# Input projection of a two-layer hybrid backbone: the low halves of the weights formed on VectorE, and the PSUM copies and head-norm steps given a place 100 instructions earlier in the planner's order

## The chip, the cores and the metric

The kernel runs on one core of one Trainium2 chip. The metric is device time in microseconds (us) of one execution of the whole program; lower is better. The program is one launch: both layers, the attention, the long convolution, the feed-forward and the last norm.

## What the reference computes

Two trunk layers run over 1152 tokens of width 1024: 128 context tokens and 1024 latent tokens, each group with its own modulation. What matters here is the first half of a layer:

```python
h = _rms_norm(x, p['norm1']) * (1 + sc1) + sh1
proj = h @ p['w_in']                                   # 1024 -> 2048 columns
q, k, v, zc, zh = jnp.split(proj, IN_SPLITS, axis=-1)  # 512, 128, 128, 512, 768
q = _rms_norm(q.reshape(b, L, N_HEADS, HEAD_DIM), p['q_norm'])
k = _rms_norm(k.reshape(b, L, N_KV_HEADS, HEAD_DIM), p['k_norm'])
q = _rope_2d(q, rows, cols); k = _rope_2d(k, rows, cols)
attn_out = _blocked_attention(q, keys, vals)
conv_out = _conformer_conv(zc, p)     # a * sigmoid(gate), 31 taps, group norm, silu, projection
hy_out = _hyena(zh, p)                # 3-tap conv, then two long convolutions with gates
x = x + g1 * (jnp.concatenate([attn_out, conv_out, hy_out], axis=-1) @ p['w_o'])
```

The other half is a feed-forward of width 2816 with a 3-tap convolution. All of it is float32.

## The kernel before

**Precision.** Every large matrix product is made of three products of rounded halves (`mm3`): high weight by high activation, high weight by low activation, low weight by high activation. A weight piece of 128x512 is loaded by a DMA of SyncE's queue into `raw` (two buffers), ScalarE casts it to `whi`, and an engine named by `self.wl_eng` subtracts to get `wlo` (four buffers each; `wload`, lines 257 to 265). `wqueue` issues the load of a piece two pieces ahead of its use.

**Stage.** `phase1` is the input projection of a layer. The 2048 columns are 16 blocks `m` of 128, taken in the order 10 to 15 (the long convolution's inputs), 0 (q), 4 (k), 5 (v), 1 (q), 8, 6, 9, 7 (the gated convolution's two pairs), 2, 3 (q). A block takes two weight pieces; its result is three PSUM tiles of 384 tokens (`dense`, or `normed_dense2` for the first two blocks, where the norm of the input is worked out segment by segment). In `phase1`, `self.wl_eng` is GpSimd; `phase3` and `phase4` set it to VectorE.

**What follows a block.** Blocks 10 to 15 are copied by ScalarE into one padded row `raw` (`short`, four copies, after three GpSimd memsets of the padding) and run through three taps into `zs`. Blocks 0 to 4 are squared and scaled by ScalarE out of PSUM (`nsq`, `nw`), head sums are made on TensorE (`s`, `sums64`), ScalarE takes the root and VectorE the reciprocal (`nsd`), TensorE spreads it (`nr`, `bcast64`) and VectorE multiplies (`nw`); `rope_out` follows, with two products on GpSimd. Block 5 is copied out (`vraw`). Blocks 8 and 9 go through a tanh (`th`), and with 6 and 7 still in PSUM VectorE forms the product (`do_glu`). The tiles of `s` and `nr` share a single PSUM buffer (`self.A`); the projection's own PSUM ring has four tiles.

**Beside it.** Between the parts of a block, `tick` takes one step of the head norms (`post`) and one of the long convolution (`bg`: `hyena`, two transforms of a chain of VectorE additions and products between TensorE products `ft`, `xp`, `iy`). In layer 0 the filter's transform (`pre`) runs first. After block 9 the long convolution is run to its end, its memory is given up, and `open_attention` takes the memory for keys and queries; `maxes(0)`, the first stage of the attention, runs beside blocks 7, 2 and 3.

**Order.** The program is written once in this order; a planner then gives each engine its own in-order list, from a simulated timeline. Among instructions that are ready in that timeline the one that stands earliest in the program goes first, and `tc.high_priority(offset=n)` makes an instruction count as n places earlier. Nothing is reordered on the chip: each engine takes its list in order.

Of the kernel before, what the change touches and what calls it, by code (L numbers as in the profile page):

```python
# [11 lines left out]
AF = mybir.ActivationFunctionType  # L12
ALU = mybir.AluOpType
# [109 lines left out]

SIDE_TAPS = 10

ORDER = [([10, 11, 12, 13, 14, 15, 0, 4, 5, 1, 8, 6, 9, 7, 2, 3], 9), ([10, 11, 12, 13, 14, 15, 0, 4, 5, 1, 8, 6, 9, 7, 2, 3], 9)]

MX_LAG = 1
# [6 lines left out]
class Kern:  # L135
# [87 lines left out]

    def stt(self, out, a, s, b, op0, op1, eng=None):
        return (eng or self.nc.vector).scalar_tensor_tensor(out, a, s, b, op0=op0, op1=op1)  # L225

    def hilo(self, hi, lo, src, hi_eng="act", lo_eng=None):

        if hi_eng == "act":
            self.nc.scalar.copy(hi, src)  # L230
        else:
            hi_eng.tensor_copy(hi, src)
        self.tt(lo, src, hi.bitcast(F32), ALU.subtract, lo_eng)
# [487 lines left out]
    def short(self, l, m, ts):  # L721

        nc, v = self.nc, self.vec[l]
        raw = self.hs.tile([128, 1156], F32, tag="raw", name="raw", bufs=1)
        nc.gpsimd.memset(raw[:, 0:1], 0.0)
        nc.gpsimd.memset(raw[:, 129:130], 0.0)
        nc.gpsimd.memset(raw[:, 1154:1155], 0.0)
        nc.scalar.copy(raw[:, 1:129], ts[0][:, 0:128])
        nc.scalar.copy(raw[:, 130:386], ts[0][:, 128:384])
        nc.scalar.copy(raw[:, 386:770], ts[1][:, 0:384])  # L730
        nc.scalar.copy(raw[:, 770:1154], ts[2][:, 0:384])
        z = self.hs.tile([128, 1156], F32, tag="zs", name="zs", bufs=3)
        w = V_SW + 3 * m
        self.act(z[:, :1153], raw[:, 1:1154], AF.Identity, scale=v[:, w + 1 : w + 2], bias=v[:, V_SB + m : V_SB + m + 1])
        self.stt(z[:, :1153], raw[:, 0:1153], v[:, w : w + 1], z[:, :1153], ALU.mult, ALU.add)
        self.stt(z[:, :1153], raw[:, 2:1155], v[:, w + 2 : w + 3], z[:, :1153], ALU.mult, ALU.add)
        self.dump(f"z{l}", z[:, :1153], lambda d: d[:, m, :])
        return z
# [323 lines left out]
    def normed(self, l, ts, w, scale, eps, done, dst):  # L1062

        nc, ms, qs = self.nc, [], []
        for s, t in enumerate(ts):
            q = self.N("nsq", "nsq", 3)
            self.act(q[:], t[:, :384], AF.Square)
            qs.append(q)
            m = self.N("nw", "nw", 4)
            self.act(m[:], t[:, :384], AF.Copy, scale=w)  # L1070
            ms.append(m)
        yield
        sd = self.small([128, 9, 2], "nsd")
        self.act(sd[:], self.sums64(qs), AF.Sqrt, scale=scale, bias=eps)
        nc.vector.reciprocal(sd[:], sd[:])
        yield
        for s in range(3):
            R = self.bcast64(sd, 3 * s, 3 * s + 3, "nr")
            self.mul(ms[s][:], ms[s][:], R[:, :384])
            if s == 0:  # L1080
                done(ms[0][:, 0:128])
            self.rope_out(l, ms[s], s, dst)
            yield
# [20 lines left out]
    def do_v(self, l, ts):  # L1104
        nc = self.nc

        ms = []
        for s in range(3):
            m = self.N("vraw", "nw", 4)
            nc.scalar.copy(m[:], ts[s][:, :384])  # L1110
            ms.append(m)
        nc.sync.dma_start(self.o["nv"][l], ms[0][:, 0:128])
        yield
        blocks = [(s, b) for s in range(3) for b in range(3)]
        for g in ((0,), (1, 2, 3, 4), (5, 6, 7, 8)):
            t = self.A("vt")
            for k, n in enumerate(g):
                s, b = blocks[n]
                self.tr(t[:, 128 * k : 128 * k + 128], ms[s][:, 128 * b : 128 * b + 128])
            if len(g) == 1:  # L1120
                m = self.M("vp")
                nc.scalar.copy(m[:, :128], t[:, :128])
                nc.sync.dma_start(self.vpD[:], m[:, :128])
            else:
                m = self.M("vs")
                nc.scalar.copy(m[:], t[:])
                nc.sync.dma_start(self.vD[:, g[0] - 1 : g[0] + 3].rearrange("p b g e -> p (b g e)"), m[:])
            yield

    def do_gate(self, ts):  # L1130
        ms = []
        for t in ts:
            m = self.N("th", "nw", 4)
            self.act(m[:], t[:, :384], AF.Tanh, scale=0.5)
            ms.append(m)
        return ms

    def do_glu(self, l, c, th, ta):

        for s, (a, b) in enumerate(SEG):  # L1140
            self.stt(th[s][:], th[s][:], 1.0, ta[s][:, :384], ALU.add, ALU.mult)
            self.nc.sync.dma_start(self.uD[c, :, a:b], th[s][:])

    def open_short(self):
# [3 lines left out]
    def phase1(self, l, x, pre):  # L1148

        nc = self.nc  # L1150
        with ExitStack() as ctx:
            with self.tc.high_priority(offset=P4_PRIO[0] + 40):
# [1 line left out]
                hp = self.pool(ctx, f"h{l}", 8)  # L1154
                hh = [hp.tile([128, NT], F32R, tag="hh", name="hh") for _ in range(8)]
                hl = [hp.tile([128, NT], F32R, tag="hl", name="hl") for _ in range(8)]
            self.wl_eng = nc.gpsimd
            self.rp = self.pool(ctx, f"rp{l}", 1)
            main = self.ring(ctx, f"p{l}", 2, 4)
            self.use(main)  # L1160
            order, end = ORDER[l]
            w = self.wqueue([self.i["w_in"][l, m, h] for m in order for h in range(2)])
# [9 lines left out]
            for k, m in enumerate(order):  # L1172
                ts = next(two) if k < 2 else self.dense(w, hh, hl, "win", tick=tick)
# [696 lines left out]
```

## Time and profile before

| | us |
|---|---|
| three timed runs: lowest, median, highest | 3380.13, 3380.18, 3384.11 |
| the profiled execution, its own time | 3374.35 |
| span of that execution's trace | 3372.2 |
| TensorE matmul busy in the span | 3159.7 (94%) |
| VectorE busy | 2166.0 (64%) |
| ScalarE busy | 1193.9 (35%) |
| GpSimd busy | 626.8 (19%) |

Around the span lie 3374.35 - 3372.2 = 2.15 us. TensorE's busy time is the sum of pipelined matmuls and not a measure of peak; what counts below is the time in which it has nothing at all, and the granted clock. Layer 0's projection runs from about 88 to 394 us, layer 1's from about 1760 to 2048 us.

### The profile page before, as it was taken

What the parts mean: (1) busy time and instruction counts of PE and PEld (TensorE: products, weight loads), DVE (VectorE), ACT (ScalarE), POOL (GpSimd) and SP (SyncE); (2) the same over time, 40 slices, a digit from 0 to 9 for tenths busy, and PEclk for the clock granted to TensorE, in tenths of its full rate; (3) what the DMA queues carried; (4) which work ended last, traced back from release to release, by engine and by line L of the source; (5) the groups of instructions that cost most, each with busy time, mean ns of one, the idle gap of its engine ahead of it and who ended that gap; (6) DMA issues with size and microseconds to landing.
All of it is one profiled execution on the core that took longest, in us unless ns stands there. A gap on an engine that the chain in (4) does not pass through costs nothing.

```text
span 3372.2 us, 44662 instructions
## 1 busy us (share of the span) xinstructions
PE 3159.7 (94%) x17330; PEld 2782.6 (83%) x17330; DVE 2166.0 (64%) x3398; ACT 1193.9 (35%) x1978; POOL 626.8 (19%) x478
## 2 busy tenths in 40 slices
PE   5999778999899999999999998889999999999997
PEld 3899733459799999999999995335799999999997
DVE  7878799665765545455477786897356444554556
ACT  3433333452342223333344333335334233333323
POOL 6533324231210000000024333332110000000002
PEclk8899879999899999999999997889999999999998
DMA  7565544544311111111123536341511111111112
GB/s 284 172 210 184 144 155 165 172 149 155 125 38 42 44 42 44 41 45 41 44 79 104 188 116 207 109 152 51 197 32 48 41 43 43 41 44 41 41 45 69
DMA packets 152327, 336.08 MB, mean 100 GB/s; under 512 B 21360, under 2 KB 57844, under 8 KB 145589
## 3 DMA queue, kind: packets, MB, share of 16 engines
q1 hardware_dynamic: 147412, 318.69, 29.5%
q0 software_dynamic: 4704, 14.55, 1.5%
q8 instruction: 137, 2.24, 0.3%
q14 instruction: 74, 0.60, 0.1%
HBM read 264.86 MB, written 68.31 MB: 99 GB/s over the span
## 4 chain that ended last, share of the span: by engine, by line
PE 72%; DVE 17%; DMA 6%; issue 2%; ACT 1%; POOL 1%; SPq 1%; DVEq 0%; ACTq 0%; POOLq 0%
PE up L236 32%; PE dn L236 16%; PE win L236 6%; PE wo L236 6%; DVE ca L225 3%; PE av L236 2%; PE st L236 2%; DVE mx L1343 2%; PE S L236 2%; DVE nt L225 1%; DMA q<-qD 1%; DVE Y L213 1%; PE fc L236 1%; DVE hl L225 1%; PE flt L236 1%
## 5 line engine op out<-in xcount | busy, mean ns | idle before, releaser
L236 PE MATMUL up<-hl,whi 128*128 128x384 f32 (+1 forms) x2112 | 713.1, 338 | 4.2 <-DVE hl L225 3.4
L236 PE MATMUL up<-hh,whi 128*128 128x384 f32 (+1 forms) x2112 | 711.0, 338 | 3.6 <-ACT hh L210 2.7
L236 PE MATMUL up<-hh,wlo 128*128 128x384 f32 (+1 forms) x2112 | 712.0, 337 | 0.0
L213 DVE TENSOR_TENSOR wlo<-wraw,whi 128x512 fp32r<-128x512 f32 x296 | 205.7, 695 | 626.1 <-ACT whi L230 623.7
L230 ACT CAST whi<-wraw 128x512 fp32r<-128x512 f32 x362 | 223.9, 619 | 835.5 <-PE dn L236 358.1
L236 PEld LDWEIGHTS up<-hl,whi 128*128 128x128 f32 x2112 | 399.0, 189 | 6.2 <-DVE hl L225 4.9
L236 PEld LDWEIGHTS up<-hh,whi 128*128 128x128 f32 x2112 | 399.0, 189 | 4.3 <-ACT hh L210 3.1
L236 PEld LDWEIGHTS up<-hh,wlo 128*128 128x128 f32 x2112 | 399.0, 189 | 0.0
L225 DVE SCALAR_TENSOR_TENSOR xt<-dn,mod,xt 128x128 f32<-128x128 f32 (+2 forms) x704 | 332.3, 513 | 71.7 <-PE dn L236 71.5
L236 PE MATMUL dn<-gh,wlo 128*128 128x384 f32 (+1 forms) x1056 | 359.0, 340 | 0.0
L236 PE MATMUL dn<-gh,whi 128*128 128x384 f32 (+1 forms) x1056 | 358.1, 339 | 0.0
L213 POOL TENSOR_TENSOR acc<-acc,sq 128x384 f32<-128x384 f32 x51 | 55.7, 1102 | 1625.2 <-ACT sq L210 1624.3
L236 PE MATMUL dn<-gl,whi 128*128 128x384 f32 (+1 forms) x1056 | 357.4, 338 | 0.0
L225 DVE SCALAR_TENSOR_TENSOR fu<-pd,vec,fu 128x1154 f32<-128x1154 f32 (+2 forms) x192 | 254.0, 1324 | 91.7 <-ACT fu L210 89.2
L236 PE MATMUL win<-hh,whi 128*128 128x384 f32 x768 | 267.6, 350 | 7.2 <-DVE th L225 2.9
L236 PE MATMUL win<-hl,whi 128*128 128x384 f32 x768 | 267.3, 349 | 6.0 <-POOL hl L213 2.4
L236 PE MATMUL win<-hh,wlo 128*128 128x384 f32 x768 | 267.0, 348 | 0.5 <-POOL wlo L213 0.5
L1343 DVE TENSOR_REDUCE mx<-S 128x1 f32<-128x384 f32 x384 | 195.7, 548 | 55.6 <-PE S L236 54.8
L1664 ACT COPY pd<-up 128x384 f32<-128x384 f32 (+1 forms) x352 | 131.8, 401 | 238.1 <-PE up L236 238.1
L210 ACT ACTIVATE p<-st 128x1024 f32<-128x1024 f32 x144 | 147.1, 1021 | 168.1 <-PE st L236 167.7
L236 PEld LDWEIGHTS dn<-gl,whi 128*128 128x128 f32 x1056 | 199.9, 189 | 0.0
L236 PEld LDWEIGHTS dn<-gh,whi 128*128 128x128 f32 x1056 | 199.7, 189 | 0.0
(295 smaller groups left out, 5405.6 us busy)
## 6 DMA issues: line engine op xcount, KB each, us to landing
wmod<-in_w_mod SPq DMA_DIRECT2D x48, 1024.0 KB
wraw<-in_w_up SPq DMA_DIRECT2D x176, 256.0 KB
wraw<-in_w_dn SPq DMA_DIRECT2D x88, 256.0 KB
wraw<-in_w_in SPq DMA_DIRECT2D x64, 256.0 KB
q<-qD SPq DMA_DIRECT2D x48, 256.0 KB
mh<-mixD SPq DMA_DIRECT2D x16, 576.0 KB
ml<-mixD SPq DMA_DIRECT2D x16, 576.0 KB
khD<-fK SPq DMA_DIRECT2D x16, 512.0 KB
```

What stands on the lines that cost most here:

```text
L210: return self.nc.scalar.activation(out, in_, f, **k)
L213: return (eng or self.nc.vector).tensor_tensor(out, a, b, op=op)
L225: return (eng or self.nc.vector).scalar_tensor_tensor(out, a, s, b, op0=op0, op1=op1)
L230: self.nc.scalar.copy(hi, src)
L236: self.nc.tensor.matmul(out, l, r, start=start, stop=stop)
L1343: nc.vector.tensor_reduce(m3[:, k, s : s + 1], S[:, :384], op=ALU.max, axis=AX.X)
L1664: self.nc.scalar.copy(p[:, u + o : v + o], t[:, u - a : v - a])
```

## The change

The engine of `wlo` in `phase1` becomes VectorE. A new `soon()` lets the instructions inside it count as 100 places earlier. It is put around the copies of `short`, the square and the scaled copy of `normed`, its root and reciprocal, its product with the spread reciprocal, the copies of `do_v`, the tanh of `do_gate` and the product of `do_glu`. Matmuls, DMAs, memsets, `rope_out` and the weight casts keep their places. `normed` gets one more empty `yield` between the reciprocal and the first `bcast64`, so the spread is issued one tick (a part of 12 matmuls) later.

```diff
+OUT_PRIO = 100
+    def soon(self):
+        return self.tc.high_priority(offset=OUT_PRIO)
@@ short
-        nc.scalar.copy(raw[:, 1:129], ts[0][:, 0:128])
...
+        with self.soon():
+            nc.scalar.copy(raw[:, 1:129], ts[0][:, 0:128])
+            nc.scalar.copy(raw[:, 130:386], ts[0][:, 128:384])
+            nc.scalar.copy(raw[:, 386:770], ts[1][:, 0:384])
+            nc.scalar.copy(raw[:, 770:1154], ts[2][:, 0:384])
@@ normed
+            with self.soon():
+                q = self.N("nsq", "nsq", 3)
+                self.act(q[:], t[:, :384], AF.Square)
+                qs.append(q)
+                m = self.N("nw", "nw", 4)
+                self.act(m[:], t[:, :384], AF.Copy, scale=w)
+                ms.append(m)
         yield
         sd = self.small([128, 9, 2], "nsd")
-        self.act(sd[:], self.sums64(qs), AF.Sqrt, scale=scale, bias=eps)
-        nc.vector.reciprocal(sd[:], sd[:])
+        t = self.sums64(qs)
+        with self.soon():
+            self.act(sd[:], t, AF.Sqrt, scale=scale, bias=eps)
+            nc.vector.reciprocal(sd[:], sd[:])
+        yield
         yield
         for s in range(3):
             R = self.bcast64(sd, 3 * s, 3 * s + 3, "nr")
-            self.mul(ms[s][:], ms[s][:], R[:, :384])
+            with self.soon():
+                self.mul(ms[s][:], ms[s][:], R[:, :384])
@@ do_v
+            with self.soon():
+                m = self.N("vraw", "nw", 4)
+                nc.scalar.copy(m[:], ts[s][:, :384])
@@ do_gate
+            with self.soon():
+                m = self.N("th", "nw", 4)
+                self.act(m[:], t[:, :384], AF.Tanh, scale=0.5)
@@ do_glu
-            self.stt(th[s][:], th[s][:], 1.0, ta[s][:, :384], ALU.add, ALU.mult)
+            with self.soon():
+                self.stt(th[s][:], th[s][:], 1.0, ta[s][:, :384], ALU.add, ALU.mult)
@@ phase1
-            self.wl_eng = nc.gpsimd
+            self.wl_eng = nc.vector
```

## Rows read from the trace of the kernel before

**Rows 1.** Windows: length; PE, PEld, DVE, ACT, POOL busy; clock; DMA share; GB/s.

```profile
187.00:394.00 207.00, 197.30 (x1281) 190.00 (x1281) 174.04 (x269) 73.69 (x133) 63.64 (x56) 0.97 0.53 169
...
1750.00:1795.00 45.00, 37.14 (x178) 33.16 (x177) 42.58 (x65) 29.65 (x63) 26.19 (x26) 0.85 0.55 199
1795.00:2048.00 253.00, 243.06 (x1547) 235.55 (x1546) 182.35 (x280) 88.28 (x160) 90.86 (x72) 0.99 0.45 142
```

**Rows 2.** Timelines around the two hand-overs to the attention: DVE and PE.

```profile
393.23 1.27 DVE L213 TENSOR_TENSOR hyo<-y2t,g 128x128 f32<-128x128 f32 x4 [0.66 <-PE y2t L246]
...
420.59 1.30 PE L236 MATMUL S<-k,q 128*128 128x384 f32 x3 [4.82 <-issue]
...
2023.25 1.33 DVE L213 TENSOR_TENSOR hyo<-y2t,g 128x128 f32<-128x128 f32 x4 [4.50 <-PE y2t L246]
```

**Rows 3.** The projection's tile `win`: matmuls, first and last start.

```profile
L236 PE MATMUL win<-hh,wlo x768: 333/336/742, 93.6 to 2047.7; 128*128 128x384 f32 x192
```

**Rows 4.** What PE waited for, 187 to 410 us: total, times, longest.

```profile
PE nr L236 <- DVE nw L213: 4.1, 2, 3.4
...
PE s L236 <- DVE nw L213: 3.1, 2, 1.7
```

**Rows 5.** The same, 1795 to 2065 us.

```profile
PE nr L236 <- DVE nsd L1075: 3.0, 1, 3.0
PE win L236 <- DVE th L225: 2.9, 1, 2.9
PE nr L236 <- DVE nw L213: 1.6, 1, 1.6
```

**Rows 6.** Windows around one stall of PE (columns as in Rows 1).

```profile
1967.00:1971.00 4.00, 1.10 (x15) 0.85 (x12) 4.00 (x8) 0.00 (x0) 0.10 (x1) 0.99 0.06 16
1971.00:1975.00 4.00, 4.00 (x16) 4.00 (x15) 3.94 (x8) 2.42 (x4) 1.77 (x2) 0.58 0.16 53
```

**Rows 7.** SyncE's queue, what it waited for: 80 to 400, then 1795 to 2050 us.

```profile
SPq L263 <- POOL wlo L213: 55.1, 20, 6.8
...
SPq L263 <- POOL wlo L213: 83.4, 21, 20.2
```

**Rows 8.** Timelines of POOL, SP and DVE at two long `wlo` instructions.

```profile
172.04 1.27 DVE L225 SCALAR_TENSOR_TENSOR fK<-fsd,fE 128x512 f32<-128x512 f32 x2
...
167.38 7.69 POOL L213 TENSOR_TENSOR wlo<-wraw,whi 128x512 fp32r<-128x512 f32 x1
...
175.10 0.33 SPq L263 DMA_DIRECT2D wraw<-in_w_in  x1
...
1844.69 11.58 POOL L213 TENSOR_TENSOR wlo<-wraw,whi 128x512 fp32r<-128x512 f32 x1 [6.07 <-ACT whi L230]
...
1838.64 17.98 SPq L263 DMA_DIRECT2D wraw<-in_w_in  x2
...
1862.87 1.23 DVE L213 TENSOR_TENSOR W<-X,khat 128x1024 f32<-128x1024 f32 x1 [2.48 <-DMA khat<-khD]
```

**Rows 9.** Tile `wlo`: ns min/median/max of one on each engine.

```profile
L213 DVE TENSOR_TENSOR wlo<-wraw,whi x296: 670/691/1839, 371.6 to 3320.5; 128x512 fp32r<-128x512 f32 x148
L213 POOL TENSOR_TENSOR wlo<-wraw,whi x66: 1260/1463/11579, 40.4 to 2020.8; 128x512 fp32r<-128x512 f32 x66
```

**Rows 10.** The long convolution's DVE steps, 187 to 394 us: ns min/median/max.

```profile
L213 DVE TENSOR_TENSOR Y<-Y,W x16: 621/679/1778, 225.9 to 351.5; 128x512 f32<-128x512 f32 x16
...
L213 DVE TENSOR_TENSOR pqmn<-d x8: 411/414/1503, 257.9 to 364.8; 128x256 f32<-128x256 f32 x8
```

**Rows 11.** What POOL waited for, 187 to 394 us.

```profile
POOL wlo L213 <- ACT whi L230: 67.6, 16, 12.2
```

**Rows 12.** Costliest groups of the whole span: busy, mean ns, idle before.

```profile
L213 DVE TENSOR_TENSOR wlo<-wraw,whi 128x512 fp32r<-128x512 f32 x296 | 205.7, 695 | 626.1 <-ACT whi L230 623.7
```

**Rows 13.** Windows, tile `wlo` alone: PE, PEld, DVE, POOL busy (count); clock, DMA.

```profile
187.00:394.00 207.00, 91.80 (x268) 51.16 (x268) 1.39 (x2) 36.95 (x21) 0.97 0.53 169
...
1795.00:2048.00 253.00, 121.34 (x355) 67.52 (x354) 1.37 (x2) 62.83 (x29) 0.99 0.45 142
```

More of the change, by code (lines that the diff above doesn't have):

```diff
@@ L727, in short @@
         nc.gpsimd.memset(raw[:, 1154:1155], 0.0)
-        nc.scalar.copy(raw[:, 1:129], ts[0][:, 0:128])
-        nc.scalar.copy(raw[:, 130:386], ts[0][:, 128:384])
-        nc.scalar.copy(raw[:, 386:770], ts[1][:, 0:384])
-        nc.scalar.copy(raw[:, 770:1154], ts[2][:, 0:384])
+        with self.soon():
[3 more added lines that the diff above has]
+            nc.scalar.copy(raw[:, 770:1154], ts[2][:, 0:384])
         z = self.hs.tile([128, 1156], F32, tag="zs", name="zs", bufs=3)
@@ L1065, in normed @@
         for s, t in enumerate(ts):
[L1066 to L1071, printed above, removed]
+            with self.soon():
[5 more added lines that the diff above has]
+                ms.append(m)
         yield
         sd = self.small([128, 9, 2], "nsd")
-        self.act(sd[:], self.sums64(qs), AF.Sqrt, scale=scale, bias=eps)
-        nc.vector.reciprocal(sd[:], sd[:])
+        t = self.sums64(qs)
[3 more added lines that the diff above has]
+        yield
         yield
@@ L1108, in do_v @@
         for s in range(3):
-            m = self.N("vraw", "nw", 4)
-            nc.scalar.copy(m[:], ts[s][:, :384])
+            with self.soon():
+                m = self.N("vraw", "nw", 4)
+                nc.scalar.copy(m[:], ts[s][:, :384])
             ms.append(m)
@@ L1132, in do_gate @@
         for t in ts:
-            m = self.N("th", "nw", 4)
-            self.act(m[:], t[:, :384], AF.Tanh, scale=0.5)
+            with self.soon():
+                m = self.N("th", "nw", 4)
+                self.act(m[:], t[:, :384], AF.Tanh, scale=0.5)
             ms.append(m)
```

## Prediction

> **What bounds the kernel now.** I began with busy time by stretches of the two projection stages, since only they change. In layer 0, from the long convolution's start to the last projection matmul (187 to 394 us), TensorE is without work for 207 - 197.3 = 9.7 us and its granted clock is 0.97, which costs another 0.03 x 207 = 6.2 us; in layer 1 (1795 to 2048 us) it is 9.9 us idle and 0.01 x 253 = 2.5 us of clock [rows 1]. So TensorE is the bound, and 15.9 us and 12.4 us are all that can be got inside these stretches. VectorE is second: 174 of 207 us and 182 of 253 us [rows 1], and it carries the serial chain of the long convolution.
>
> Then I asked what releases the stage after, the attention. In layer 0 the last step of the long convolution (`hyo`) ends at 394.5 us and the first score matmul `S` starts at 420.59, after a wait for the loads that follow the convolution's output [rows 2]. So in layer 0 the convolution sets the end, and TensorE's time counts only where it delays the convolution. In layer 1 `hyo` ends at 2024.6 us, and projection matmuls go on to 2047.7 [rows 2, 3]: 23 us of slack for the convolution, and every us of TensorE counts. Both must be kept apart in the sum.
>
> Next, TensorE's waits. In layer 1 two are of the kind that the change speaks of: 2.9 us for `do_glu`'s product (`th`), which frees the PSUM tiles, and 3.0 us for the reciprocal `nsd`; the spread `nr` waits 1.6 us more for the product `nw` at the end [rows 5]. In layer 0 the head sums `s` wait twice for `nw`, 3.1 us together, and `nr` twice, 4.1 us [rows 4]. A stall has a second cost: after the 2.9 us one the granted clock is 0.58, close to the lower of the two levels (1.2 of 2.4 GHz), for 4 us [rows 6], so 0.42 x 4 = 1.7 us are lost once more.
>
> Last, SyncE's queue. It waited 55.1 us in layer 0 and 83.4 us in layer 1 to issue a weight load, because GpSimd had not finished the `wlo` that reads the old `raw` buffer [rows 7]. One such instruction took 7.69 us and one 11.58 us [rows 8], against a median of 1.46 [rows 9]. Behind the second, SyncE stands 17.98 us, and the filter spectrum `khat` queued after it reaches VectorE 2.48 us late [rows 8].
>
> **The change, part by part.**
>
> *`wlo` on VectorE.* One takes 0.691 us there [rows 9]. In layer 0's stretch 21 move, in layer 1's 29 [rows 13]: 14.5 and 20.0 us more for VectorE. Against this stands what GpSimd's instructions cost VectorE now. Steps of the convolution that take 0.679 and 0.411 us in the median take up to 1.778 and 1.503 [rows 10]: 1.1 us more when they collide. Per `wlo` moved that is a relief between nothing and 1.1 us; I take the middle, 0.55, because the median of these steps is undisturbed and not every `wlo` meets one. Net: 21 x (0.691 - 0.55) = +3.0 us on layer 0's convolution (ends: +14.5 and 21 x (0.691 - 1.1) = -8.6). In layer 1 the same, +4.1 us, lies inside the 23 us of slack and costs nothing; without the slack it would cost its 4.1.
>
> The Trainium skill (SBUF — State Buffer, Who interferes with whom) says that a VectorE instruction with two SBUF inputs and a GpSimd one that reads SBUF exclude each other, and that the later one is blocked for the whole of the first. By that rule, with GpSimd's shortest `wlo` of 1.26 us as the block, the relief would be 1.26 and the net 21 x (0.691 - 1.26) = -11.9 us in place of +3.0; I return to it among the rivals.
>
> *SyncE and GpSimd.* With `raw` freed by a 0.7 us instruction the long holds go. In layer 0 the last filter spectrum is formed at 173.3 us, but SyncE is held until 175.10 [rows 8]: the convolution, which waits for these stores to give up memory, can start 1.8 us sooner. In layer 1 the late `khat` is again inside the slack: nothing. GpSimd keeps its memsets of `raw`'s padding, rope products and constant loads, none of which then stands behind a `wlo`; I count nothing for it, as TensorE waits for none of them in rows 4 and 5.
>
> *Copies and products 100 places earlier.* No instruction is added. On ScalarE the copies, squares and tanhs go ahead of convolution copies and weight casts that are ready with them; ScalarE is busy 88 of 253 us [rows 1], so most already go at once. On VectorE, which is fuller, `nw`, `nsd` and `th` go ahead of convolution steps of 0.4 to 0.7 us [rows 10]. DMAs keep their places: SyncE's list changes only where its inputs come sooner. What is passed is the convolution, which lies behind four short VectorE instructions per head-norm block and three per gate block; they run before its end now too, so over the stage it loses nothing by it.
>
> Layer 1: `th` 2.9 + 1.7 of clock; `nsd` 3.0 + 1.7 (the extra tick takes the reciprocal off the way even if the planner misjudges it, and the next products come a tick later behind projection matmuls, which cover it); final `nw` 1.6. Together 10.9. A new order makes stalls of its own, between nothing and as many as the old one had; I take off 3. Layer 1: -7.9.
>
> Layer 0: -1.8 for the earlier start; of the two `s` waits the one inside the convolution's stretch, 3.1 - 1.7 = 1.4, with 1.7 of clock: -3.1; VectorE's net +3.0. The other `s` wait and the 4.1 us of `nr` lie around the end, beside the loads that hold `S` until 420.59: nothing; if those loads came at once they would be worth 1.7 + 4.1 = 5.8. Layer 0: -1.9.
>
> Sum: -7.9 - 1.9 = -9.8 us. The profiled execution took 3374.35 us, so 3364.5 by its own time. It was faster than the three timed runs, whose median is 3380.18; I put the difference on the median: 3370 us. About 0.2% (6.8 us) is what a measurement of this kernel can tell from no change, so "faster" begins at 3373.4 and "slower" at 3386.9.
>
> **The rivals.**
>
> *The order hardly changes.* Priority acts only among instructions that are ready together in the planner's timeline. With ScalarE at a third [rows 1], most copies already go at once, and the two stalls of layer 1 may come from that timeline being wrong, which priority doesn't mend. Against: the extra tick acts in any case. What is left is the 1.8 us of layer 0's start: 3378 us.
>
> *Larger gain.* All of TensorE's idle time and lost clock goes, in layer 0 because the convolution, with GpSimd off its way, runs 12 us sooner (the -11.9 above) and 1.8 and 3.1 more: 16.8, which covers the 15.9 that TensorE can give. With 12.4 + 1.6 in layer 1 that is 30 us: 3350 us. For it speak the 7.69 and 11.58 us blocks [rows 8]: GpSimd does stand still whole. Against it: the convolution's steps are undisturbed in the median [rows 10], and head sums, `yp` and `iy` have waits of their own. The Trainium skill's rule on the shared port (SBUF — State Buffer, Who interferes with whom) would bring this case about.
>
> *Slower: VectorE held at `wlo`.* VectorE takes its list in order. A `wlo` waits for ScalarE's cast, and that for TensorE to finish with a buffer; behind it stand the convolution's steps, `nw`, `nsd` and `th`, for which TensorE waits. GpSimd stood 67.6 us before its `wlo` for the cast in layer 0 [rows 11], 3.2 us for each of 21; in the stages where `wlo` is on VectorE, it stands 623.7/296 = 2.1 us [rows 12]. VectorE has 33 us of idle time in layer 0's stretch [rows 1], 1.6 us per `wlo`; holds beyond that come onto the convolution. With the rest of my sum, the change turns slower than before from 21h - 33 - 1.9 = 7.9, a hold h of 2.04 us. Halfway between the two rows, at 2.65, the convolution ends 22.7 us later for it: 3380 - 9.8 + 22.7 = 3393 us. Against it: both rows are of engines that had little else in their list at that time, and a list from a simulated timeline puts the `wlo` where the cast should be done. [...]
>
> **How the numbers follow.** My forecast, a gain of 7 to 22 us (3358 to 3373), 0.43; the larger gain 0.15; hardly any change 0.24; slower 0.18. Faster is then 0.58, the same 0.24, slower 0.18. The range of 8 in 10 has to reach into the cases of both signs: from 3350 (half of the larger gain lies below) to 3390 (half of the slower case lies above), which leaves out 0.17. VectorE's ends, -8.6 and +14.5 in place of +3.0, lie in it: 3358 and 3382.
>
> **What would show it.** Right: no GpSimd `wlo` in either stage; SyncE's waits for `wlo` a small part of 55.1 and 83.4; no wait of the projection for `th` or of `nr` for `nsd` over 1 us in layer 1, and the clock of its stretch at 1.00; the last projection matmul of layer 1 some 8 us earlier after the stage's start; `hyo` in layer 0 ending about 2 us earlier. Wrong: VectorE idle before `wlo` for the cast by more than 40 us in layer 0; `hyo` ending later there, with the same wait up to `S`; or a new order in which TensorE stands for the convolution (`iy`, `y2t`) as long as it did for `th` and `nsd`.

## The result, and the profile after

The changed kernel takes 3344.66 us (median of 4 runs, 3341.96 to 3348.25) where the kernel before takes 3380.57 (4 runs on the same chip, 3380.13 to 3384.11). The ratio is 0.9897, with a 95% interval of 0.9884 to 0.9909: faster by about 35 us. The forecast was 3370, its range 3350 to 3390: the sign was right, and the gain is more than three times the forecast one; the time lies below the range. The profiled execution took 3345.59 us with a span of 3343.3, so the two traces differ by 28.9 us; the one of before had come out 6 us below the median. By stages the 28.9 us are 4.4 up to the output projection of layer 0 (`wo`), 1.6 from there to layer 1's projection, 13.6 in it, 7.7 in layer 1's attention and 1.6 behind that.

The stages first. The next two blocks are windows of the kernel before and of the changed one, cut at the projections' last matmul and at the first matmul of the output projection (`wo`); the columns are those of [rows 1].

```profile
88.80:392.40 303.60, 287.82 (x1755) 275.43 (x1756) 249.59 (x370) 114.85 (x214) 118.69 (x100) 0.95 0.54 174
392.40:754.00 361.60, 309.57 (x1382) 151.14 (x1380) 275.42 (x489) 147.96 (x214) 124.62 (x74) 0.87 0.49 163
1762.80:2047.70 284.90, 268.73 (x1653) 257.30 (x1654) 214.25 (x328) 109.22 (x204) 110.07 (x91) 0.96 0.47 150
2047.70:2400.50 352.80, 308.13 (x1324) 150.63 (x1323) 282.67 (x478) 145.69 (x210) 120.17 (x65) 0.87 0.40 130
```

```profile
94.20:383.60 289.40, 278.92 (x1712) 266.34 (x1713) 241.59 (x385) 110.41 (x205) 63.72 (x71) 0.97 0.55 175
383.60:749.60 366.00, 309.19 (x1413) 152.67 (x1411) 277.90 (x497) 150.08 (x217) 126.94 (x74) 0.87 0.49 164
1756.80:2028.10 271.30, 262.06 (x1652) 253.38 (x1653) 215.69 (x358) 108.91 (x202) 38.12 (x52) 0.98 0.44 143
2028.10:2373.20 345.10, 296.56 (x1308) 147.19 (x1308) 275.05 (x476) 146.44 (x211) 121.72 (x73) 0.90 0.46 146
...
1790.00:2028.10 238.10, 237.79 (x1544) 232.34 (x1543) 184.26 (x306) 88.52 (x157) 21.60 (x35) 1.00 0.42 135
```

In layer 1's projection the matmul count is the same (1653, 1652) and the time 13.6 us less: TensorE's idle time fell from 284.9 - 268.7 = 16.2 us to 9.2, and its busy time by 6.7 us, since the granted clock rose. From 1790 us on it is idle for 0.3 us of 238 at a clock of 1.00, all of it at the upper of the two levels (2.4 GHz); the stretch that answers to it was idle for 9.9 us at 0.99 [rows 1]. GpSimd's busy time fell from 110 to 38 us; VectorE's hardly moved (214.3 to 215.7), although some 30 low parts were added to it. Layer 0's projection ends at 383.6 us in place of 392.4, of which the attention gives back 4.4. Layer 1's attention, in which no line of the code changed, is 7.7 us shorter: TensorE is idle there a little longer than before (48.5 us, 44.7 before), but its busy time, for nearly the same matmuls (1308, 1324), fell by 11.6 us at a clock of 0.90 in place of 0.87.

What TensorE waited for, in the changed kernel, from 1790 to 2065 us and then from 187 to 410 us (total, times, longest):

```profile
PE s L241 <- DVE nw L215: 3.9, 1, 3.9
PE S L241 <- issue: 3.4, 1, 3.4
...
PE nr L241 <- DVE nw L215: 1.5, 2, 0.9
PE nr L241 <- DVE nsd L1084: 0.7, 1, 0.7
...
PE iy L241 <- ACT zh L235: 2.2, 1, 2.2
PE nr L241 <- DVE nw L215: 1.9, 2, 1.2
```

The waits of 2.9 us for `th` and 3.0 us for `nsd` of [rows 5] are gone, or down to 0.7. The 3.9 us for `s` stand behind the last projection matmul, at 2029 us: part of the old tail now falls into the next stage. How the attention is reached, in timelines of the changed kernel (VectorE and TensorE in layer 0, then in layer 1), answering to [rows 2], and the last projection matmul, to [rows 3]; the last line is layer 1's first score matmul in the kernel before:

```profile
391.02 1.26 DVE L215 TENSOR_TENSOR hyo<-y2t,g 128x128 f32<-128x128 f32 x4
...
414.57 1.30 PE L241 MATMUL S<-k,q 128*128 128x384 f32 x3 [8.14 <-DMA k<-kD]
...
2019.34 1.30 DVE L215 TENSOR_TENSOR hyo<-y2t,g 128x128 f32<-128x128 f32 x4 [1.95 <-PE y2t L251]
...
2046.66 1.30 PE L241 MATMUL S<-k,q 128*128 128x384 f32 x3 [3.44 <-issue]
```

```profile
L241 PE MATMUL win<-hh,wlo x768: 333/336/742, 96.4 to 2028.1; 128*128 128x384 f32 x192
...
2047.87 0.70 PE L236 MATMUL S<-k,q 128*128 128x384 f32 x3
```

In layer 1 the scores start 2046.7 - 1756.8 = 289.9 us after the stage's start; before it was 2047.9 - 1762.8 = 285.1. The projection ends 13.6 us earlier and the scores do not start earlier: between the two, from 2028.1 to 2046.7, TensorE is busy for 9.1 of 18.6 us. What was gained lies behind this point: most of the tail of the q heads (head sums `s`, spreads `nr`) runs in this gap, where in the kernel before it came behind the first scores.

### The profile page after: what moved, and what is told of

The parts are those of the page before. It is cut to its first block, busy times and chain, and to the rows that moved or that the text cites. A ratio compares the mean times of both kernels' runs of the same rounds, so it can differ in the third digit from the quotient of the medians.

```text
span 3343.3 us, 44669 instructions
## 1 busy us (share of the span) xinstructions
PE 3134.0 (94%) x17330; PEld 2769.0 (83%) x17330; DVE 2160.7 (65%) x3464; ACT 1195.1 (36%) x1976; POOL 495.1 (15%) x412
## 5 line engine op out<-in xcount | busy, mean ns | idle before, releaser
L215 DVE TENSOR_TENSOR wlo<-wraw,whi 128x512 fp32r<-128x512 f32 x362 | 255.6, 706 | 646.6 <-ACT whi L235 646.3
L227 DVE SCALAR_TENSOR_TENSOR fu<-pd,vec,fu 128x1154 f32<-128x1154 f32 (+2 forms) x192 | 254.0, 1324 | 91.7 <-ACT fu L212 89.2
L241 PE MATMUL win<-hh,wlo 128*128 128x384 f32 x768 | 263.8, 344 | 0.0
```

What stands on the lines that cost most here:

```text
L215: return (eng or self.nc.vector).tensor_tensor(out, a, b, op=op)
L241: self.nc.tensor.matmul(out, l, r, start=start, stop=stop)
```

## The experiments

The table holds all runs that the text speaks of: the ratio of times to the kernel before (95% interval), and from each profile the start of layer 0's last projection matmul, the length of layer 0's attention up to `wo`, of layer 1's projection (first to last matmul) and of layer 1's attention up to `wo`, all in us. "Low" is the low parts on VectorE, "places" the earlier places with the extra tick.

| | ratio | layer 0: projection's end | attention | layer 1: projection | attention |
|---|---|---|---|---|---|
| before | 1 | 392.4 | 361.6 | 284.9 | 352.8 |
| the change (low, places) | 0.9897 (0.9884 to 0.9909) | 383.6 | 366.0 | 271.3 | 345.1 |
| 1: low alone | 0.9929 (0.9913 to 0.9945) | 386.5 | 365.4 | 271.2 | 350.1 |
| 2: places alone | 0.9975 (0.9964 to 0.9986) | 391.9 | 359.8 | 284.9 | 352.2 |
| 3: the change in layer 0 | 0.9963 (0.9950 to 0.9976) | 385.2 | 361.1 | 288.5 | 351.5 |
| 4: the change in layer 1 | 0.9947 (0.9930 to 0.9964) | 395.3 | 361.6 | 270.0 | 354.5 |
| 5: before, loads on GpSimd's queue | 1.0033 (1.0023 to 1.0043) | 397.5 | 356.6 | 292.1 | 362.3 |
| 6: low, 2 idle subtractions | 0.9967 (0.9954 to 0.9980) | 389.5 | 365.9 | 276.6 | 358.0 |
| 7: low, 4 idle subtractions | 1.0088 (1.0071 to 1.0105) | 412.3 | 364.9 | 290.8 | 355.9 |
| 8: low, 2 idle copies | 0.9963 (0.9948 to 0.9978) | 383.0 | 372.8 | 271.2 | 357.0 |
| 9: the change, no tick | 0.9899 (0.9884 to 0.9913) | 383.5 | 364.8 | 269.6 | 342.4 |
| 10: low, places of head norms | 0.9897 (0.9882 to 0.9912) | 386.2 | 368.0 | 270.2 | 346.3 |
| 11: the change, every 5th | 0.9906 (0.9891 to 0.9921) | 383.7 | 363.7 | 270.3 | 344.0 |
| 12: the change, every 7th | 0.9926 (0.9909 to 0.9942) | 384.6 | 363.7 | 270.1 | 349.1 |
| 13: low alone, every 5th | 0.9890 (0.9876 to 0.9905) | 382.7 | 360.6 | 269.5 | 345.3 |
| 14: low alone, every 7th | 0.9917 (0.9902 to 0.9932) | 385.4 | 363.9 | 269.9 | 348.8 |
| 15: the change, `cz` on VectorE | 0.9945 (0.9930 to 0.9959) | 384.8 | 365.1 | 269.8 | 358.9 |
| 16: the change, first `es` on VectorE | 0.9940 (0.9919 to 0.9960) | 382.9 | 354.9 | 270.4 | 354.3 |

One trace is good to a few us: runs 1, 3, 9 and 10 and the change have the same lists in layer 0's attention, and it took 361.1 to 368.0 us.

### Which part of the change: runs 1 to 4

Run 1, the low parts alone:

```diff
-            self.wl_eng = nc.gpsimd
+            self.wl_eng = nc.vector
```

> The low parts on VectorE alone, without the priorities and without the extra tick. In layer 0 each engine's list is then the same as in the changed kernel, so all theories expect layer 0's projection at about 289 us there (303.6 before). Theory A, the engine of the low parts carries the gain: layer 1's projection at 271 to 275 us (284.9 before, 271.3 after), in all 3344 to 3352 us. Theory B, the priorities carry layer 1: its projection stays at 281 to 285 us, its attention at about 353, in all 3366 to 3376 us. Theory C, the gain in layer 1's attention (352.8 to 345.1 us) comes from the order that the planner happens to find there, and belongs to no part: the attention lies anywhere from 340 to 358 us, apart from what the projection does.

Run 2 is the changed kernel with that line put back to `nc.gpsimd`.

> The priorities and the extra tick, with the low parts left on GpSimd. The lists of layer 0 are the same as before on every engine; a few hundred instructions of layer 1 stand elsewhere. Theory A, the engine of the low parts carries the gain: layer 1's projection at 281 to 286 us as before, in all 3376 to 3384 us. Theory B, the priorities carry layer 1: its projection at 272 to 277 us, in all 3350 to 3365 us. Theory C, layer 1's attention goes with the order found: it may lie at 340 to 358 us with no relation to its projection.

Runs 3 and 4 hold the whole change in one layer:

```diff
     def soon(self):
-        return self.tc.high_priority(offset=OUT_PRIO)
+        return self.tc.high_priority(offset=OUT_PRIO) if self.lay == 0 else ExitStack()
...
-            self.wl_eng = nc.vector
+            self.wl_eng = nc.vector if l == 0 else nc.gpsimd
```

> The whole change in layer 0 alone; layer 1 has its low parts on GpSimd and no priorities. The stages of the changed kernel's layer 0 sum to about -6 us by the trace (head +5.3, projection -14.2, attention +4.4, the output projection +1.2, feed-forward -2.8). Theory A and B: layer 1 as before, in all 3371 to 3376 us. Theory C: layer 1's list is planned anew behind the changed layer 0, and its attention moves by several us though nothing in its code changed: 3362 to 3386 us, with layer 1's projection still at 283 to 287 us.

> The whole change in layer 1 alone; layer 0 as before. Theory A and B: layer 0 at 303.6 us for its projection, layer 1 as in the changed kernel (projection 271, attention 345): 22 to 30 us less than before, 3350 to 3358 us. Theory C: the projection gives its 13.6 us, of which the hand-over keeps part, and the attention lies anywhere: 3345 to 3375 us.

The projections are clear. With the low parts on VectorE layer 1's takes 269.5 to 271.3 us in all eleven kernels that have the low parts on VectorE in that layer and no idle work added, with and without the places; with them on GpSimd it takes 284.9 to 292.1 (four kernels). The places alone leave it at 284.9. They do take `th` off the path and put another wait in its stead. TensorE's waits of run 2, 1795 to 2060 us:

```profile
PE nr L241 <- DVE nw L215: 4.2, 3, 2.0
...
PE win L241 <- DVE th L227: 0.7, 1, 0.7
PE nr L241 <- DVE nsd L1084: 0.2, 1, 0.2
```

In layer 0 the places change nothing: each engine's list is the same without them. So Theory A holds for the projections. Run 2's ratio of 0.9975 has no counterpart in its trace, where layer 1 is 0.6 us shorter up to `wo` and layer 0, with the same lists as before, 2.3; what these 8 us are stays open. Run 1's total, 3357.22, lies above A's range, and run 4's attention took 354.5 us against 345.1 in the changed kernel, with the same code in layer 1: layer 1's attention speaks for C, and runs 11 to 14 return to it.

### Why VectorE does it better: runs 5 to 8

Run 5 leaves the low parts on GpSimd and takes the hold off SyncE:

```diff
-        nc.sync.dma_start(raw[:], src)
+        (nc.gpsimd if self.wl_eng is nc.gpsimd else nc.sync).dma_start(raw[:], src)
```

> The kernel before, with one edit: in the two projections the weight loads are issued from GpSimd's queue and not from SyncE's. The low parts stay on GpSimd, so VectorE has neither more nor less to do and meets GpSimd as before, but SyncE no longer stands for the old raw buffer. Theory Hold, the gain of 23 us of the low parts on VectorE is that SyncE's queue is free: projections at 290 to 294 us in layer 0 and 271 to 275 in layer 1, 3352 to 3360 us in all. Theory Share, the gain is that GpSimd no longer works beside VectorE for 1.3 to 11.6 us at a time: projections at 301 to 306 and 282 to 287 us, 3376 to 3384 us.

It came out slower, 1.0033: freeing SyncE gave nothing. The projections, 307.0 and 292.1 us, lie above the ranges of both theories. The edit has a cost of its own, 0.57 us of GpSimd for each of these loads, so it alone doesn't decide. The two rows of its GpSimd from 90 to 397 us (busy, mean ns | idle before):

```profile
L213 POOL TENSOR_TENSOR wlo<-wraw,whi 128x512 fp32r<-128x512 f32 x29 | 64.2, 2216 | 59.6 <-ACT whi L230 59.5
L263 POOL DMA_DIRECT2D wraw<-in_w_in x26 | 14.7, 566 | 4.9 <-POOL wlo L213 3.6 <-PE win L236 0.9 <-PE ft L236 0.3
```

The changed kernel itself speaks against Hold. SyncE's waits there, 180 to 400 us and 1760 to 2050 us:

```profile
SPq L268 <- DVE wlo L215: 32.0, 17, 7.8
...
SPq L268 <- DVE wlo L215: 90.4, 26, 15.4
```

In layer 1 SyncE waits for the low parts as long as before (83.4 us [rows 7]), now for VectorE's, and the projection is 13.6 us shorter all the same. Nor does TensorE wait for any load in layer 1's projection in either kernel, and ScalarE's casts wait for a weight piece 1.7 us before and 3.4 us in the changed kernel. VectorE's one wait for a late load, 2.5 us for `khat` [rows 8], is gone, and that is what is left to Hold. So a shorter hold is not what gave most of the time.

Where part of it was lost shows in the steps that lead to `th`. VectorE of the kernel before, and GpSimd beside it (start, us):

```profile
1958.06 3.31 DVE L213 TENSOR_TENSOR Y<-Y,W 128x512 f32<-128x512 f32 x2
...
1963.57 1.28 DVE L225 SCALAR_TENSOR_TENSOR X<-jk,p 128x512 f32<-128x512 f32 x2
...
1969.91 0.54 DVE L225 SCALAR_TENSOR_TENSOR th<-th,win 128x384 f32<-128x384 f32 x1
...
1953.97 6.86 POOL L213 TENSOR_TENSOR wlo<-wraw,whi 128x512 fp32r<-128x512 f32 x2 [10.34 <-ACT whi L230]
```

The same steps in the changed kernel:

```profile
1949.61 1.23 DVE L215 TENSOR_TENSOR Y<-Y,W 128x512 f32<-128x512 f32 x2
1950.75 1.23 DVE L215 TENSOR_TENSOR W<-X,khat 128x1024 f32<-128x1024 f32 x1
1951.89 1.22 DVE L215 TENSOR_TENSOR Y<-X,khat 128x1024 f32<-128x1024 f32 x1
1953.02 1.29 DVE L227 SCALAR_TENSOR_TENSOR X<-jk,p 128x512 f32<-128x512 f32 x2
1954.23 0.69 DVE L215 TENSOR_TENSOR wlo<-wraw,whi 128x512 fp32r<-128x512 f32 x1
...
1959.97 0.56 DVE L227 SCALAR_TENSOR_TENSOR th<-th,win 128x384 f32<-128x384 f32 x1
```

One pair `Y` takes 3.31 us where GpSimd is in the middle of two low parts, and 1.23 us where it is not: 2.1 us, at a place from which the chain runs without a gap to `th`, for which TensorE waited 2.9 us and after which its clock fell [rows 6]. In the changed kernel that stretch has a low part of 0.69 us more on VectorE, and TensorE's wait for `th` is 0.3 us.

Run 6 puts GpSimd's work back without its use. The low parts stay on VectorE, and per weight piece GpSimd makes two subtractions whose result nobody reads:

```diff
         self.hilo(wh[:], wl[:], raw[:], lo_eng=self.wl_eng)
+        if self.shadow:
+            for p in (0, 256):
+                s = self.rp.tile([128, 256], mybir.dt.bfloat16, tag="wsh", name="wsh", bufs=1)
+                self.tt(s[:], wh[:, p : p + 256].bitcast(F32), wh[:, p : p + 256].bitcast(F32), ALU.subtract, nc.gpsimd)
```

> The low parts on VectorE alone (as in the run that took 3357 us), and for every weight piece of the projections two subtractions of GpSimd on 128x256 of the high part, into a tile that nobody reads. The raw buffer is free after VectorE's 0.7 us as before, so SyncE isn't held; GpSimd works about as much beside VectorE as before the change. Theory Hold: projections at 290 to 294 and 271 to 275 us, 3354 to 3361 us. Theory Share: VectorE has the low parts and the collisions too, projections at 300 us or more and 280 us or more, 3375 to 3395 us.

Run 7 makes four of them per piece (`for p in (0, 256, 0, 256)`).

> The low parts on VectorE alone, and now four idle subtractions of GpSimd per weight piece in the projections in place of two. With two, the kernel took 3372 us against 3357 without, and VectorE's instructions were longer by 15.2 and 14.2 us in the two projections where they met these subtractions. Theory Share: as much again, projections at 300 to 304 and 281 to 286 us, 3380 to 3395 us. If what the first two took back was an accident of the order: no further loss, 3366 to 3376 us.

Run 8 makes two copies in place of the two subtractions (`nc.gpsimd.tensor_copy(s[:], wh[:, p : p + 256].bitcast(F32))`).

> As the run with two idle subtractions per piece, but GpSimd copies the high part (one tile read, one written) in place of subtracting (two read, one written). If VectorE is held by GpSimd's two reads alone: the loss goes away, 3354 to 3361 us, projections 290 to 293 and 271 to 273 us. If GpSimd's work holds it whatever it reads: 3367 to 3376 us, projections at 296 and 276 us.

The steps that lead to `th` in run 6, and GpSimd beside them:

```profile
1957.31 1.96 DVE L214 TENSOR_TENSOR Y<-Y,W 128x512 f32<-128x512 f32 x2
1959.19 1.63 DVE L214 TENSOR_TENSOR W<-X,khat 128x1024 f32<-128x1024 f32 x1
1960.75 1.63 DVE L214 TENSOR_TENSOR Y<-X,khat 128x1024 f32<-128x1024 f32 x1
...
1969.25 0.55 DVE L226 SCALAR_TENSOR_TENSOR th<-th,win 128x384 f32<-128x384 f32 x1
...
1952.78 8.52 POOL L214 TENSOR_TENSOR wsh<-whi 128x256 bf16<-128x256 f32 x4 [11.09 <-ACT whi L231]
```

The same in run 8:

```profile
1952.82 1.51 DVE L214 TENSOR_TENSOR Y<-Y,W 128x512 f32<-128x512 f32 x2
1954.25 1.41 DVE L214 TENSOR_TENSOR W<-X,khat 128x1024 f32<-128x1024 f32 x1
1955.59 1.41 DVE L214 TENSOR_TENSOR Y<-X,khat 128x1024 f32<-128x1024 f32 x1
...
1948.26 5.52 POOL L269 CAST wsh<-whi 128x256 bf16<-128x256 f32 x2 [12.04 <-ACT whi L231]
```

And TensorE's waits for `th` in runs 6, 7 and 8, in that order, each from the table of waits of layer 1's projection:

```profile
PE win L237 <- DVE th L226: 1.7, 1, 1.7
```

```profile
PE win L237 <- DVE th L226: 3.1, 1, 3.1
PE yp2t L247 <- DVE hyo L214: 2.8, 1, 2.8
```

```profile
PE win L237 <- DVE th L226: 0.8, 1, 0.8
```

Run 1, the same code without idle work, has no wait for `th`, and the eleven kernels of that kind have none to 1.0 us; with two subtractions per piece it is 1.7, with four 3.1. The 0.8 us beside copies can't be told from none. The three steps of VectorE shown take 1.23, 1.23 and 1.22 us in the changed kernel, 1.96, 1.63 and 1.63 beside subtractions, and 1.51, 1.41 and 1.41 beside copies. Layer 1's projection takes 271.2, 276.6 and 290.8 us with none, two and four, and 271.2 beside copies. The closest pair are runs 6 and 8: from 40 us into layer 1's projection up to `wo`, every engine takes the same instructions in the same order in both, the idle work aside. So Share is shown as a cause: GpSimd's subtractions beside VectorE's chain make TensorE wait, with the low parts on VectorE. SyncE waits for the low parts about as long in both, 97.7 and 94.8 us. The windows from 1795 us to the end of layer 1's projection in runs 1, 6 and 8, and SyncE's wait in run 6:

```profile
1795.00:2031.10 236.10, 235.82 (x1537) 230.38 (x1536) 185.56 (x309) 88.22 (x158) 23.16 (x37) 1.00 0.42 135
1795.00:2039.60 244.60, 242.31 (x1557) 236.05 (x1557) 201.66 (x314) 91.17 (x167) 92.79 (x94) 0.99 0.42 131
1795.00:2032.70 237.70, 236.32 (x1539) 230.71 (x1538) 191.74 (x308) 87.37 (x156) 77.49 (x93) 1.00 0.43 135
...
SPq L264 <- DVE wlo L214: 97.7, 31, 18.1
```

Two subtractions took back 276.6 - 271.2 = 5.4 of the 13.7 us between before and run 1 in layer 1, and 3.0 of 5.9 in layer 0. The 5.4 us are 2.6 us of TensorE's idle time (10.8 in run 6, 8.2 in run 1) and 2.8 us of its busy time, at a clock of 0.96 in place of 0.97. From 1795 us on, where `th` is, it is idle for 2.3 us in run 6 and 0.3 in run 1. Neither theory's forecast of run 6 was met: 296.9 and 276.6 us lie between the ranges of Hold and of Share, so the effect is there and smaller than forecast. Run 7, at 320.3 and 290.8 us, lies beyond Share's ranges; run 8's projections, 290.8 and 271.2 us, are those forecast if GpSimd's two reads alone hold VectorE, its total is not. The four cost more than twice the two; in layer 0 TensorE waits elsewhere too (5.1 us before `flt`, 3.9 for `hh`), so run 7 is no pure dose. The copies cost no projection time. Run 8 is still above run 1, 0.9963 to 0.9929, with both attentions 7 us longer; no copies run there. In layer 1's attention runs 6 and 8 share one list, another than run 1's, and took 358.0 and 357.0 us, which points at the list.

The other 8.3 us in layer 1 go with waits that run 6 does not have again inside the stage (in the kernel before 3.0 us for `nsd` [rows 5], 1.3 at `yp`, 1.0 at `iy`) and with their clock. The longest, `nsd`, is no collision. In the kernel before, ScalarE takes the root for it behind casts `mh` of the convolution's output, and these wait for stores; GpSimd runs nothing from 2027.2 to 2041.2 us. ScalarE there:

```profile
2034.48 0.62 ACT L230 CAST mh<-hyo 128x512 fp32r<-128x512 f32 x1 [3.01 <-DMA mixD<-ml]
...
2037.67 0.28 ACT L210 ACTIVATE nsd<-s,eps 128x18 f32<-128x18 f32 x1
```

So this wait goes with the order of ScalarE's list, and the tail of the head norms to which it belongs only moved behind the last projection matmul. How much of the rest is GpSimd's lateness and how much the order of the lists was not told apart.

### Layer 1's attention: runs 9 to 14

Run 9 drops the extra tick, run 10 keeps the earlier places (and the tick) for `normed` alone.

> The changed kernel without the extra tick between the reciprocal and the spread. In the lists only 65 of 16206 TensorE instructions and 85 of 3436 of VectorE stand elsewhere, all in layer 1. If the priorities beside the low parts are what takes the kernel from 3357 to 3345 us: 3343 to 3349 us. If layer 1's attention merely falls as its list happens to fall: it may lie at 342 to 356 us, 3343 to 3358 us in all.

> The low parts on VectorE, the tick, and the earlier places for the head norms' instructions alone (not for the copies of the long convolution's inputs, the tanhs, the gate's products or v). The projection of layer 1 then has the list that it has with the low parts alone, the attention of layer 1 nearly the list of the run without the tick. If the attention's list decides: as the run without the tick, within 4 us. If the earlier copies in the projection decide: as the low parts alone, 3354 to 3360 us.

Both are as fast as the change, 0.9899 and 0.9897. That alone would fit a gain from the head norms' earlier places. Runs 11 to 14 change one number that leaves every list of both projections as it is and re-plans the attentions, with the places (11, 12) and without (13, 14):

```diff
-P2_TAPS, TAPS_PRIO = 6, 300
+P2_TAPS, TAPS_PRIO = 5, 300
```

> The changed kernel, with a step of the gated convolution at every 5th step of its taps in place of every 6th: both projections keep their lists, both attentions get others; the work is the same. If the earlier places speed up layer 1's attention: 342 to 348 us for it here and in the run with every 7th, and 349 to 355 in the two runs without the earlier places. If the attention goes with the list: both sides spread over the same 342 to 358 us, and layer 0's attention, which has the same list on both sides, moves by several us from 366 too.

> The changed kernel, every 7th step. Earlier places help: layer 1's attention at 342 to 348 us. The list alone: anywhere from 342 to 358 us.

> The low parts on VectorE alone, every 5th step. Earlier places help: layer 1's attention at 349 to 355 us here, above the two runs with them. The list alone: anywhere from 342 to 358 us, and as likely below those.

> The low parts on VectorE alone, every 7th step. Earlier places help: layer 1's attention at 349 to 355 us. The list alone: anywhere from 342 to 358 us, and as likely below the runs with the earlier places.

Without the places run 13 reaches 0.9890, the lowest ratio of all; with them run 12 has 0.9926. Layer 1's attention takes 342.4 to 349.1 us in five kernels with the places (run 10 has part of them) and 345.3 to 350.1 in three without; run 4, with the places in layer 1, took 354.5. The mean ratio is 0.9905 with and 0.9912 without. The places are worth nothing that these runs can tell from the draw of the list. Whether the low parts shorten this attention stays open: the eight kernels with them on VectorE in both layers and no other work moved lie at 342.4 to 350.1 us, the three with them on GpSimd in layer 1 and the loads as before at 351.5 to 352.8, but run 4, which has them on VectorE in layer 1, at 354.5.

### Does the lesson carry: runs 15 and 16

Run 15 takes the side sum of the gated convolution off GpSimd, run 16 the first of each row of sums of exponentials:

```diff
-                    self.add(Z[:], Z[:], y[:], nc.gpsimd)
+                    self.add(Z[:], Z[:], y[:])
```

```diff
-                self.add(part[k][:], ..., P[:], None if k else nc.gpsimd)
+                self.add(part[k][:], ..., P[:], None if k or c < 4 else nc.gpsimd)
```

> The changed kernel, and in both attentions the 18 additions of 128x584 of the gated convolution's side sum on VectorE in place of GpSimd. VectorE's instructions are longer by 11.4 and 10.2 us where they meet these additions; one addition of this shape takes 0.76 us on VectorE, 13.7 us for 18. If the relief of the projection carries over: VectorE's net is +2 to +4 us in each attention, less than what the order alone moves, so 3340 to 3352 us. If GpSimd's share counts for more than its collisions: 3325 to 3338 us. If VectorE, at 275 of 345 us, is held up by its longer list: 3353 to 3370 us.

> The changed kernel, and in both attentions the first of each row of sums of exponentials (8 additions of 128x1024) on VectorE in place of GpSimd. They lengthen VectorE's instructions by 4.7 and 10.6 us; 8 of this shape take 10.4 us on VectorE. If the relief carries over: VectorE's net is +6 us in layer 0 and nothing in layer 1, 3342 to 3355 us. If GpSimd's share counts for more: 3328 to 3340 us.

Both are slower than the change, 0.9945 and 0.9940 to 0.9897: layer 1's attention takes 358.9 and 354.3 us. Layer 0's is no longer than in the changed kernel, 365.1 and 354.9 us to 366.0. In the attention VectorE is itself what TensorE waits for (`mx` and `nmx`, 24.6 us in layer 1 of the changed kernel), but the longer list doesn't show as longer waits: in run 15 these two come to 18.9 us, and what grew is TensorE's busy time, 309.2 us in place of 296.6, at a clock of 0.87 in place of 0.90. Other lists of the unchanged attention took 342.4 to 362.3 us. So the moves brought no gain, and whether they cost anything beyond the new order was not told apart. No kernel beat the change; run 13 equals it.

## Why the prediction was wrong, step by step

**The step that failed.** For layer 1 the prediction priced the low parts at nothing ("lies inside the 23 us of slack and costs nothing") and credited the 10.9 us of waits to the earlier places. It is the other way round: the low parts alone gave 13.7 us of layer 1's projection and the places alone 0.0 (runs 1 and 2). At least a part of it is GpSimd's work beside VectorE's chain, of which two idle subtractions per piece took 5.4 us back (run 6). The waits for `th` and `nsd` were seen, with their clock [rows 5, 6], and so were GpSimd's blocks [rows 8]; that the wait for `th` stood at the far end of a chain with a step lengthened beside such a block was not. The pair of 3.31 us stands in VectorE's timeline ahead of `th`. And the wait for `nsd`, taken for one that an earlier place of the reciprocal would end, came from casts ahead of its root in ScalarE's list; without the places it is down to 0.7 us too (run 1).

**The size of relief.** 0.55 us per low part moved was not far off on average: VectorE's busy time in layer 1's projection went from 214.3 to 215.7 us, so the relief nearly pays for the 0.69 us: +1.4 us, where 29 x (0.691 - 0.55) = 4.1 was forecast. An average says nothing of where the collisions fall: the one ahead of `th` added 2.1 us to a chain for which TensorE then waited 2.9 us, with a low clock behind it.

**The deduction of 3 us for new stalls** did not come: the stretch is down to 0.3 us idle at a clock of 1.00, which was the larger-gain rival's price for layer 1 (12.4 + 1.6 = 14.0, measured 13.6). That rival's other half failed: in layer 0 the convolution was to run 12 us sooner, and `hyo` ends at 392.3 us in place of 394.5.

**Layer 0**, -1.9 forecast, about -4 measured: `wo` starts at 749.6 us in place of 754.0, and over the five kernels with these lists at 746.3 to 754.2, against 751.7 to 757.0 in the three with the old ones. `hyo` came 2.2 us earlier as forecast (over the eleven kernels with this projection's list it ends at 391.4 to 395.3 us, in the three with the old one at 394.0 to 397.4), but by another sum: the first `ft` starts where it did (191.8 and 192.1 us), so the 1.8 us of an earlier start are not there, and the 3.0 us that VectorE was to lose were not lost. The 1.4 and 1.7 us of an `s` wait can't be the places' work either, which change no list in layer 0. The hand-over, priced at nothing, gave some 4 us: `hyo` to the first `S` took 22.3 us in place of 26.1, and it is 21.6 to 22.9 us in those eleven kernels and 24.7 to 26.1 in the three. Why it is shorter stays open.

**"The long holds go"** was wrong for layer 1: 90.4 us against 83.4. SyncE waits for the low part two pieces back on whichever engine it is.

**"Every us of TensorE counts" in layer 1** held only until the slack was used up: with 14 us gone from TensorE the scores start no earlier after the stage's start, and the gain shows in a shorter attention. `hyo` ends 263.8 us after the stage's start (261.8 before) and the scores follow it by 26.0 us, as in layer 0 they do by 22 to 26: the convolution's hand-over, and no longer TensorE, seems to set them, which no run tested. That the attention is unaffected was the second wrong assumption: it took 7.7 us less in the changed kernel, and 342 to 362 us over the runs of one and the same work.

**The extra tick** "acts in any case": alone it changes no list of any engine, and without it the change is as fast (run 9).

**The slower rival** was not met. VectorE's idle time before `wlo` is 0.5 us for each, far below the 2.04 from which it would have decided. VectorE in layer 0 from 187 to 384 us and in layer 1 from 1790 to 2028 us:

```profile
L215 DVE TENSOR_TENSOR wlo<-wraw,whi 128x512 fp32r<-128x512 f32 x22 | 15.1, 687 | 11.7 <-ACT whi L235 11.7
...
L215 DVE TENSOR_TENSOR wlo<-wraw,whi 128x512 fp32r<-128x512 f32 x30 | 21.0, 699 | 14.5 <-ACT whi L235 14.4
```

Of its signs, those for `th`, `nsd`, the clock of 1.00 and GpSimd without low parts came true, and proved nothing for the places, since run 1 shows them too.

The rule of the Trainium skill (SBUF — State Buffer, Who interferes with whom) that a VectorE instruction with two SBUF inputs and a GpSimd one that reads SBUF exclude each other points at the cause that the runs found. As a price it was too high here: -11.9 us for layer 0's convolution, where 2.2 came. And it makes no difference between GpSimd's copies and subtractions, both of which read SBUF; runs 6 and 8 show one, 5.4 us against none in layer 1's projection.

## What to carry to other kernels

Where a matmul waits for a VectorE step, read VectorE's timeline backwards from that step and compare each duration with its group's median: a step well above its median beside a GpSimd instruction is a suspect, which idle GpSimd work put back can test, and moving that work can pay even when VectorE's busy total does not fall. Judge a priority by what it changes in each engine's list before pricing it; here it changed none in layer 0. When a change re-plans a stage that it does not touch, draw that stage's order a few times with and without the change before crediting the change with its time: here it moved by as much as the earlier places seemed to give.

## What the runs showed that was not expected

GpSimd copies of 128x256 cost VectorE less than subtractions of the same size: `W` and `Y` took 1.41 us beside copies, 1.63 beside subtractions and 1.23 alone. The copies were themselves held: two took 5.52 us at 1948 us, against a mean of 0.85 each in layer 0's projection. Which side is held changes within a few us: in the kernel before and in runs 6 and 8, `W` and `Y` ahead of the reciprocal `nsd` take their usual 1.21 to 1.23 us although GpSimd's instruction is already running beside them, and the lengthened steps start right behind `nsd`. Why there was not tested. And executions of one list differ by up to 7 us in one stage (361.1 to 368.0 in layer 0's attention), more than many edits are worth.
